# A hybrid decoder layer: the state-space outputs by channels instead of by tokens

## The chip, the cores and the metric

The kernel runs on one core of a Trainium2 chip. The metric is the device time of one execution in microseconds (us).

## What is computed

One layer over 256 tokens of width 2048, in f32. The part that matters here is the state-space (SSD) group with its gate and norm:

```python
z, xbc, dt_raw, q, k, v = jnp.split(a_in @ w_in[i], [o1, o2, o3, o4, o5], axis=-1)
xbc = jax.nn.silu(_causal_dwconv(xbc, conv_w[i], conv_b[i]))
xs, bm, cm = jnp.split(xbc, ...)
dt = jax.nn.softplus(dt_raw + dt_bias[i])
# _ssd: 2 chunks of 128 tokens, 4 groups, 8 heads of 64 channels a group, state 128
y_diag = jnp.einsum('bgecls,bcsgep->bclgep', cb[:, :, None] * decay_in, X)    # X = xs * dt
y_off  = jnp.einsum('bclgn,bcgepn,bgecl->bclgep', Cc, prev, jnp.exp(a_cs))    # state carried in
y = y_diag + y_off + d_skip * xs_h
y = y.reshape(b, s, SSM_INNER) * jax.nn.silu(z)
y_ssm = _rmsnorm(y by 4 groups of 512, ssm_norm_g)
h = h + jnp.concatenate([y_ssm, y_att], axis=-1) @ w_out[i]
```

Behind it come sliding-window attention (the other half of the output projection), a feed-forward part with a convolution, and a gated embedding.

## The kernel before, in words

Every large product is a GEMM over 512 output columns. Its weights come from HBM through the SP queue, 128 x 1024 values at a time, into one of seven tiles `w`. ScalarE (ACT) casts each to a high part `wh` (L192), VectorE (DVE) subtracts to get the low part `wl` (L193), and TensorE (PE) makes three products of 128 x 512 for each slice of the contraction and each block of 128 tokens (L222 to L224). The sum stands in a pair of PSUM tiles, one for each token block, of which there are two pairs. One chunk of the input projection is eight weight tiles of twelve matmuls.

The order in which each engine gets its instructions is made ahead of the run by a planner, which follows the order of the listing where operands are ready by its own costs. The attention stage's matmuls stand in an order written by hand.

At the start the kernel projects B and C of all groups (512 columns each) and the steps dt. Then, in the listing, B and C are evacuated, convolved and put through SiLU (L424 to L429), and behind them comes the steps' chain (L431 to L474): softplus, the decay's cumulative sums, and their store to a scratch tensor `scr`, from which each group loads its rows broadcast over the partitions (`seg`, L481).

For each of four groups, `ssd_x` makes the decay matrices `seg`, multiplies them by C times B (`cb`), projects and convolves x (`xc`, by channels on the partitions), transposes `xc` to have tokens on the partitions, and scales it to `Xd`. The result `yc` is a tile for each token block, tokens on the partitions and 512 channels along it: D skip (L518), plus eight head products of 64 columns (L534), plus, in the second block, the product with the carried state `prev` (L538), scaled by `eacs`. `ssd_gate` projects z and takes its SiLU. `ssd_end` multiplies, sums the squares by rows (L558), scales by the inverse root (L561), and transposes the result back to channels on the partitions (L272), where it is split in high and low parts for the output projection (L195, L196). Group 0 is projected at once, groups 1 to 3 in the attention stage (`output`). `add_to_h` adds each product to the residual stream (L396).

In the listing of the loop, `ssd_end(g)` stands ahead of `ssd_x(g + 1)`.

Transposing by a DMA is in use already, in the attention and the feed-forward part: GpSimd (POOL) sorts the 16-bit halves of f32 values apart (`half`, L881), the SP queue issues the transfer `flip` (L883), and POOL puts the halves together again (L884).

Of the kernel before, what the change touches and what calls it, by code (L numbers as in the profile page):

```python
# [11 lines left out]
F32 = mybir.dt.float32  # L12
# [8 lines left out]
P = 128  # L21
# [44 lines left out]
def hybrid_layer(  # L66
# [330 lines left out]

    def next_lhs(lhs, ss, n, gain):

# [7 lines left out]
        V.tensor_reduce(out=s1, in_=ss, axis=AX.X, op=ALU.add)  # L407
        return rstd(s1, D, NB, tag)

    def project(lhs, w, i0, ni, after=None):  # L410

        for n in range(4):
            acc = acc_pair()
            gemm(acc, lhs, [w[i, n] for i in range(i0 * KG // KW, (i0 + ni) * KG // KW)])
            add_to_h(acc, n)
            if after:
                after(n)

# [2 lines left out]
    with tc.tile_pool(name="ssd", bufs=1) as sp, tc.tile_pool(name="dram", bufs=1, space=bass.MemoryType.DRAM) as dp:  # L421
        BT = sb(sp, [P, 4, T], "BT")
        CT = sb(sp, [P, 4, T], "CT")
        for c, (acc, dst, tag) in enumerate(((acc_b, BT, "ct"), (acc_c, CT, "Xd"))):  # L424
            t = evac_scaled(acc, sp, tag, 1)
            if c == 0:
                S.copy(dtT, dt_ps[:64, :T])
            conv_chunk(t, dst, scw, 4, 16 + 4 * c)
            S.activation(out=dst, in_=dst, func=AF.Silu)  # L429

        tr = tr_tile()  # L431
        for b in range(NB):
            PE.matmul(tr[:, b * 32 : (b + 1) * 32], lhsT=dtT[:, b * P : (b + 1) * P], rhs=sel, start=True, stop=True)
# [36 lines left out]
        V.tensor_copy(acsT, ps[:64, :P])  # L470
        scr = dp.tile([64, P], F32, tag="scr", name="scr")
        nc.sync.dma_start(scr, acsT)
        eacs = sb(sp, [P, 64], "eacs")
        S.activation(out=eacs, in_=acs, func=AF.Exp)  # L474

        def ssd_x(g):
            segs = []
            for c in range(NB):
                hs = slice(g * 16 + c * 8, g * 16 + c * 8 + 8)
                seg = sb(sp, [P, 8, P], "seg", bufs=3)  # L480
                nc.sync.dma_start(seg, scr[hs, :].partition_broadcast(P))  # L481
# [4 lines left out]
                V.tensor_tensor(out=seg, in0=seg, in1=bc(acs[:, hs], P), op=ALU.subtract)  # L486
                G.affine_select(
                    out=seg, in_=seg, compare_op=ALU.is_ge, fill=-1.0e30, base=0, pattern=[[0, 8], [1, P]], channel_multiplier=-1
                )
                S.activation(out=seg, in_=seg, func=AF.Exp)  # L490
                segs.append(seg)
# [20 lines left out]
            y, Xd = [], []  # L512
# [13 lines left out]
            PE.matmul(st, lhsT=Bt, rhs=xe, start=True, stop=True)  # L526
            prev = sb(sp, [P, NC], "prev")
            S.copy(prev, st)
            for c in range(NB):
                yc = y[c]  # L530
                yp = ms_tile()
                for h in range(8):
                    hs = slice(h * HD, (h + 1) * HD)
                    PE.matmul(yp[:, hs], lhsT=segs[c][:, h, :], rhs=Xd[c][:, hs], start=True, stop=True)  # L534
                V.tensor_tensor(out=yc, in0=yc, in1=yp, op=ALU.add)
                if c:
                    off = ms_tile()
                    PE.matmul(off, lhsT=CT[:, g, c * P : (c + 1) * P], rhs=prev, start=True, stop=True)  # L538
                    t = sb(sp, [P, NC], "xe")
                    o = g * 16 + 8  # L540
                    V.tensor_tensor(out=v3(t, 8), in0=v3(off, 8), in1=bc(eacs[:, o : o + 8], HD), op=ALU.mult)
                    V.tensor_tensor(out=yc, in0=yc, in1=t, op=ALU.add)
            return y

        def ssd_gate(g):
            acc = in_chunk(3 + 2 * g)
            zs = []
            for b in range(NB):
                z = sb(sp, [P, NC], f"z{b}")
                S.activation(out=z, in_=acc[b], func=AF.Silu, scale=rx[:, b : b + 1])  # L550
                zs.append(z)
            return zs

        def ssd_end(g, y, zs):
            ssy = sb(sp, [P, NB], "ssy", bufs=2)
            for b in range(NB):
                V.tensor_tensor(out=y[b], in0=y[b], in1=zs[b], op=ALU.mult)
                S.activation(out=zs[b], in_=y[b], func=AF.Square, accum_out=ssy[:, b : b + 1])  # L558
            ry = rstd(ssy, NC, NB, "ry")
            for b in range(NB):  # L560
                V.tensor_scalar_mul(y[b], y[b], ry[:, b : b + 1])  # L561
# [5 lines left out]
        zs = ssd_gate(0)  # L567

        with tc.tile_pool(name="rope", bufs=1) as rp:
            posf = sb(rp, [P, NB], "posf")  # L570
# [53 lines left out]
        fill(const)  # L624

        for g in range(4):
            held[g] = ssd_end(g, y, zs)
            if g < 3:
                y = ssd_x(g + 1)
                zs = ssd_gate(g + 1)  # L630
            if g < 1:
                project(*held.pop(g))


    ms_.close()
# [2 lines left out]
    with tc.tile_pool(name="att_s", bufs=2) as as_, tc.tile_pool(name="att", bufs=2, reuse_waits="tile") as ap_, tc.tile_pool(name="ps_sc", bufs=1, space=PSUM) as ps_sc:  # L638
# [130 lines left out]
        def values(j):  # L769

            yT = Lhs(yp_, KG, "y")
            for b in range(NB):
# [16 lines left out]
            held[4 + j] = (yT, w_out, 4 + j, 1)  # L789

        def chunk(c, then):
            acc = acc_pair()
# [5 lines left out]
                yield  # L798

        def output(i):  # L800
            lhs, w, i0, ni = held.pop(i)
            for n in range(4):
                acc = acc_pair()
                for s in range(2):
                    products(acc, lhs, load_w(w[i0 * 2 + s, n]), s * KW, KW, KG, s == 1)
                    if s == 1:
                        add_to_h(acc, n)
                    yield

        at = {}  # L810
# [190 lines left out]
```

## Time and profile before

| | us |
|---|---|
| median of three runs | 1434.23 (1433.61 to 1436.1) |
| the profiled execution | 1436.61 |
| its span, first to last instruction | 1434.9 |
| PE busy | 1423.2 (99%) |
| PE weight loads (PEld) busy | 1167.3 (81%) |
| DVE busy | 984.1 (69%) |
| ACT busy | 804.2 (56%) |
| POOL busy | 286.2 (20%) |

Busy time is the union of an engine's instructions. Matmuls are pipelined, so their listed durations overlap and add up to more than the time. A row of a group gives line, engine, operation, the names of output and inputs, the shapes, the count; then the busy time and the mean duration in ns of one, and the idle time just before them with what ended it. In a row of a stretch stand its limits and length, the busy time and count for PE, PEld, DVE, ACT and POOL, the granted clock of PE, the DMA share and GB/s. A row in order of time gives start, duration, engine, line and count. A row of waits gives the total, the number and the longest.

### The profile page before, as it was taken

How to read it: one execution, taken by the hardware profiler on the slowest of the kernel's cores; microseconds unless marked ns; L12 is line 12 of the kernel's file. 1: busy time of each engine (PE TensorE's matmuls, PEld its weight loads, DVE VectorE, ACT ScalarE, POOL GpSimd, SP SyncE). 2: the span in 40 equal slices, each digit the busy share in tenths (PEclk: the TensorE clock that was granted, in tenths of full speed). 3: DMA queues.
4: the chain of work that ended last, by engine and by line, in shares of the span. 5: the costliest groups of instructions: out<-in, count | busy, mean ns of one | idle time of the engine just before them, and what ended most of it. 6: DMA issues, size and time to landing. Idle time of an engine off the chain costs nothing.

```text
span 1434.9 us, 18092 instructions
## 1 busy us (share of the span) xinstructions
PE 1423.2 (99%) x6527; PEld 1167.3 (81%) x6527; DVE 984.1 (69%) x1242; ACT 804.2 (56%) x1101; POOL 286.2 (20%) x212
## 2 busy tenths in 40 slices
PE   9999999999999999999999999999999999999998
PEld 7887888888787778888888888888888888888887
DVE  6678876776678897656667646765675576476854
ACT  6675555644567666556556446545554554455643
POOL 0002010008345432013243112201320131120000
PEclk9999999999999999999999999999999999999999
DMA  9656656548687778577887767867876877776671
GB/s 332 236 173 198 215 177 185 171 148 223 188 220 187 209 220 220 168 211 207 219 226 202 217 205 206 225 196 198 230 208 192 223 201 218 206 208 190 208 226 65
DMA packets 163467, 292.62 MB, mean 204 GB/s; under 512 B 93041, under 2 KB 95921, under 8 KB 162993
## 3 DMA queue, kind: packets, MB, share of 16 engines
q1 hardware_dynamic: 162944, 290.99, 70.5%
q8 instruction: 51, 0.84, 0.2%
q10 hardware_dynamic: 432, 0.48, 0.1%
q14 instruction: 40, 0.32, 0.1%
HBM read 268.32 MB, written 2.13 MB: 188 GB/s over the span
## 4 chain that ended last, share of the span: by engine, by line
PE 68%; DVE 1%; ACT 0%; issue 0%; POOL 0%; DVEq 0%; ACTq 0%
PE acc L222 22%; PE acc L224 22%; PE acc L223 22%; PE tr L779 1%; PE tr L272 0%; PE sc L738 0%; DVE wl L193 0%; ACT s L753 0%; DVE nm L749 0%; DVE s L742 0%; ACT wh L192 0%; DVE sg L931 0%; ACT s L761 0%; DVE qkr L672 0%; DVE h L396 0%
## 5 line engine op out<-in xcount | busy, mean ns | idle before, releaser
L193 DVE TENSOR_TENSOR wl<-w,wh 128x1024 fp32r<-128x1024 f32 (+1 forms) x495 | 634.9, 1288 | 378.5 <-ACT wh L192 376.4
L192 ACT CAST wh<-w 128x1024 fp32r<-128x1024 f32 (+1 forms) x495 | 514.8, 1045 | 480.7 <-PE acc L224 431.4
L223 PE MATMUL acc<-wl,ah 128*128 128x512 f32 x1278 | 500.1, 391 | 1.5 <-DVE wl L193 1.5
L224 PE MATMUL acc<-wh,al 128*128 128x512 f32 x1278 | 499.0, 391 | 0.0
L222 PE MATMUL acc<-wh,ah 128*128 128x512 f32 x1278 | 498.3, 392 | 0.0
L223 PEld LDWEIGHTS acc<-wl,ah 128*128 128x128 f32 x1278 | 240.1, 188 | 52.3 <-DVE wl L193 2.4
L222 PEld LDWEIGHTS acc<-wh,ah 128*128 128x128 f32 x1278 | 240.1, 188 | 51.0 <-issue 1.4
L224 PEld LDWEIGHTS acc<-wh,al 128*128 128x128 f32 x1278 | 240.1, 188 | 50.1 <-issue 0.7
L224 PE MATMUL acc<-wh,gl 128*128 128x512 f32 x352 | 137.1, 390 | 0.0
L223 PE MATMUL acc<-wl,gh 128*128 128x512 f32 x352 | 137.1, 390 | 0.0
L222 PE MATMUL acc<-wh,gh 128*128 128x512 f32 x352 | 136.5, 390 | 0.0
L881 POOL COPY half<-u 128x1024 uint16<-128x1024 uint16 x44 | 62.0, 1422 | 264.3 <-ACT u L879 264.3
L222 PE MATMUL acc<-wh,yh 128*128 128x512 f32 x256 | 101.6, 397 | 0.6 <-DVE h L396 0.6
L223 PE MATMUL acc<-wl,yh 128*128 128x512 f32 x256 | 99.9, 390 | 0.0
L224 PE MATMUL acc<-wh,yl 128*128 128x512 f32 x256 | 99.7, 390 | 0.0
L884 POOL COPY uc<-flip 128x1024 uint16<-128x1024 uint16 x44 | 54.9, 1248 | 177.2 <-DMA flip<-half 174.9
L223 PEld LDWEIGHTS acc<-wl,gh 128*128 128x128 f32 x352 | 66.1, 188 | 13.7
L224 PEld LDWEIGHTS acc<-wh,gl 128*128 128x128 f32 x352 | 66.1, 188 | 13.6
L222 PEld LDWEIGHTS acc<-wh,gh 128*128 128x128 f32 x352 | 66.1, 188 | 13.6
L288 DVE SCALAR_TENSOR_TENSOR cv<-uc,fcw,cv 128x254 f32<-128x254 f32 (+1 forms) x176 | 73.2, 476 | 3.4 <-ACT cv L286 3.4
L396 DVE TENSOR_TENSOR h<-h,acc 128x512 f32<-128x512 f32 x112 | 73.0, 678 | 1.8 <-PE acc L224 1.8
L222 PEld LDWEIGHTS acc<-wh,yh 128*128 128x128 f32 x256 | 48.1, 188 | 14.6 <-issue 2.0
(239 smaller groups left out, 1129.2 us busy)
## 6 DMA issues: line engine op xcount, KB each, us to landing
w<-in_w_up_dram SPq DMA_DIRECT2D x176, 512.0 KB, 4.2
w<-in_w_in_dram SPq DMA_DIRECT2D x126, 512.0 KB, 4.2
w<-in_w_down_dram SPq DMA_DIRECT2D x88, 512.0 KB, 4.3
w<-in_w_out_dram SPq DMA_DIRECT2D x64, 512.0 KB, 4.2
w<-in_w_pg_dram SPq DMA_DIRECT2D x32, 512.0 KB, 4.3
seg<-scr SPq DMA_DIRECT2D x8, 512.0 KB, 5.0
xt<-in_xT_dram SPq DMA_DIRECT2D x16, 128.0 KB, 7.0
h<-in_x_dram SPq DMA_DIRECT2D x2, 1024.0 KB, 8.7
```

Source lines behind the costliest of these rows:

```text
L192: S.copy(hi, src)
L193: V.tensor_tensor(out=lo, in0=src, in1=hi.bitcast(F32), op=ALU.subtract)
L222: PE.matmul(acc[b], lhsT=hi, rhs=wh[:, i, :], start=(k == 0), stop=False)
L223: PE.matmul(acc[b], lhsT=hi, rhs=wl[:, i, :], start=False, stop=False)
L224: PE.matmul(acc[b], lhsT=lo, rhs=wh[:, i, :], start=False, stop=(k == total - 1 or (b == NB - 1 and k + 1 == whole)))
L288: V.scalar_tensor_tensor(out=dst[:, s:], in0=ps[:, : T - s], scalar=taps[n - 1 - s], in1=dst[:, s:], op0=ALU.mult, op1=ALU.add)
L396: V.tensor_tensor(out=hs, in0=hs, in1=acc[b], op=ALU.add)
L779: PE.matmul(v3(o[e * HD : (e + 1) * HD, kv * 2 * P : (kv + 1) * 2 * P], 2), lhsT=v[kb][:, vs], rhs=pT[e][:, :, kb, :], start=(kb == 0), st ...
L881: G.tensor_copy(half.rearrange("p (a n) -> p a n", a=2), u_.bitcast(U16).rearrange("p (n a) -> p a n", a=2))
L884: G.tensor_copy(uc[:, :, b * P : (b + 1) * P].bitcast(U16).rearrange("p f (t a) -> p f t a", a=2), flip.rearrange("p (a f) t -> p f t a", ...
```

## The change

The result of a group, `y`, now has channels on the partitions (`[128, 4, 256]`). A head's product takes a 64-column slice of `Xd` as weights and the decay matrix as the moving operand (128 columns); the two heads of a pair write the lower and upper 64 partitions of one PSUM tile. The carried state is added in the same PSUM tile, with `prev` as weights and `grown` (the exponential of the cumulative sums times C) as moving operand. D skip is one fused pass by channel over `xc`, which is in that layout already. z of groups 0 to 2 is turned to that layout with two flips through the SP queue; group 3's z is transposed on PE. The sum of squares over channels is a product with a column of ones, and the inverse root is applied when the projection is added to h. The steps' chain is listed ahead of the convolutions of B and C, and `ssd_x(g + 1)` ahead of `ssd_end(g)`.

```diff
-    def add_to_h(acc, n):
+    def add_to_h(acc, n, scale=None):
         for b in range(NB):
             hs = hres[b][:, n * NC : (n + 1) * NC]
-            V.tensor_tensor(out=hs, in0=hs, in1=acc[b], op=ALU.add)
+            if scale is None:
+                V.tensor_tensor(out=hs, in0=hs, in1=acc[b], op=ALU.add)
+            else:
+                V.scalar_tensor_tensor(out=hs, in0=acc[b], scalar=scale[:, b : b + 1], in1=hs, op0=ALU.mult, op1=ALU.add)
...
-        for c, (acc, dst, tag) in enumerate(((acc_b, BT, "ct"), (acc_c, CT, "Xd"))):
-            t = evac_scaled(acc, sp, tag, 1)
-            if c == 0:
-                S.copy(dtT, dt_ps[:64, :T])
-            conv_chunk(t, dst, scw, 4, 16 + 4 * c)
-            S.activation(out=dst, in_=dst, func=AF.Silu)
-
+        bt = evac_scaled(acc_b, sp, "ct", 1)
+        S.copy(dtT, dt_ps[:64, :T])
         tr = tr_tile()
...
         nc.sync.dma_start(scr, acsT)
-        eacs = sb(sp, [P, 64], "eacs")
-        S.activation(out=eacs, in_=acs, func=AF.Exp)
+        for c, (t, dst) in enumerate(((bt, BT), (None, CT))):
+            t = t or evac_scaled(acc_c, sp, "Xd", 1)
+            conv_chunk(t, dst, scw, 4, 16 + 4 * c)
+            S.activation(out=dst, in_=dst, func=AF.Silu)
+        skip = sb(sp, [P, 16], "skip")
+        for e_ in range(2):
+            es = slice(e_ * HD, (e_ + 1) * HD)
+            V.tensor_copy(skip[es, :], dsk[es, :].rearrange("p (f e) -> p e f", e=2)[:, e_, :])
+        ones = nc.const_aps.tensor(1.0, [P, 1], F32)
...
                     S.activation(out=dec, in_=dec, func=AF.Exp)
+                else:
+                    grown = sb(sp, [P, 8, P], "grown")
+                    S.activation(out=grown, in_=seg, func=AF.Exp)
+                    V.tensor_tensor(
+                        out=grown, in0=grown, in1=CT[:, g, P:].unsqueeze(1).to_broadcast([P, 8, P]), op=ALU.mult
+                    )
...
-                yc = sb(sp, [P, NC], f"yc{b}", bufs=2)
-                V.tensor_tensor(out=v3(yc, 8), in0=v3(tr, 8), in1=bc(dsk[:, g * 8 : (g + 1) * 8], HD), op=ALU.mult)
-                y.append(yc)
...
-            for c in range(NB):
-                yc = y[c]
-                yp = ms_tile()
-                for h in range(8):
-                    hs = slice(h * HD, (h + 1) * HD)
-                    PE.matmul(yp[:, hs], lhsT=segs[c][:, h, :], rhs=Xd[c][:, hs], start=True, stop=True)
-                V.tensor_tensor(out=yc, in0=yc, in1=yp, op=ALU.add)
-                if c:
-                    off = ms_tile()
-                    PE.matmul(off, lhsT=CT[:, g, c * P : (c + 1) * P], rhs=prev, start=True, stop=True)
-                    t = sb(sp, [P, NC], "xe")
-                    o = g * 16 + 8
-                    V.tensor_tensor(out=v3(t, 8), in0=v3(off, 8), in1=bc(eacs[:, o : o + 8], HD), op=ALU.mult)
-                    V.tensor_tensor(out=yc, in0=yc, in1=t, op=ALU.add)
+            y = sb(sp, [P, 4, T], "y", bufs=2)
+            for half in range(2):
+                yp = ms_tile().rearrange("p (a t) -> p a t", a=2)
+                own = [(0, i, Xd[0], segs[0]) for i in range(2)]
+                for i in range(2):
+                    own += [(1, i, Xd[1], segs[1]), (1, i, prev, grown)]
+                for c, i, left, right in own:
+                    for e_ in range(2):
+                        h = 4 * half + 2 * i + e_
+                        PE.matmul(
+                            yp[e_ * HD : (e_ + 1) * HD, i, c * P : (c + 1) * P],
+                            lhsT=left[:, h * HD : (h + 1) * HD],
+                            rhs=right[:, h, :],
+                            start=(left is not prev),
+                            stop=(left is not Xd[1]),
+                            skip_group_check=True,
+                        )
+                for i in range(2):
+                    f = 2 * half + i
+                    V.scalar_tensor_tensor(
+                        out=y[:, f, :], in0=xc[:, f, :], scalar=skip[:, 4 * g + f : 4 * g + f + 1], in1=yp[:, i, :], op0=ALU.mult, op1=ALU.add
+                    )
             return y
 
         def ssd_gate(g):
...
-            return zs
+            if g == 3:
+                return zs
+            zT = sb(sp, [P, 4, T], "zT")
+            for b in range(NB):
+                half = sb(sp, [P, 2 * NC], f"half{b}", U16)
+                G.tensor_copy(half.rearrange("p (a n) -> p a n", a=2), zs[b].bitcast(U16).rearrange("p (n a) -> p a n", a=2))
+                flip = zs[b].bitcast(U16).rearrange("p (a t) -> p a t", a=8)
+                nc.sync.dma_start_transpose(flip, half)
+                G.tensor_copy(
+                    zT[:, :, b * P : (b + 1) * P].bitcast(U16).rearrange("p f (t a) -> p f t a", a=2),
+                    flip.rearrange("p (a f) t -> p f t a", a=2),
+                )
+            return zT
 
-        def ssd_end(g, y, zs):
-            ssy = sb(sp, [P, NB], "ssy", bufs=2)
-            for b in range(NB):
-                V.tensor_tensor(out=y[b], in0=y[b], in1=zs[b], op=ALU.mult)
-                S.activation(out=zs[b], in_=y[b], func=AF.Square, accum_out=ssy[:, b : b + 1])
-            ry = rstd(ssy, NC, NB, "ry")
-            for b in range(NB):
-                V.tensor_scalar_mul(y[b], y[b], ry[:, b : b + 1])
-            yT = Lhs(yp_, KG, "y")
-            transpose_split(y, yT, 0, g_ssm[:, 4 * g : 4 * g + 4])
-            return (yT, w_out, g, 1)
+        def ssd_end(g, y, z):
+            if g < 3:
+                V.tensor_tensor(out=y, in0=y, in1=z, op=ALU.mult)
+            else:
+                for half in range(2):
+                    fs = slice(2 * half, 2 * half + 2)
+                    tr = tr_tile().rearrange("p (a t) -> p a t", a=2)
+                    for i in range(2):
+                        f = 2 * half + i
+                        for b in range(NB):
+                            PE.transpose(tr[:, i, b * P : (b + 1) * P], z[b][:, f * P : (f + 1) * P], ident)
+                    V.tensor_tensor(out=y[:, fs, :], in0=y[:, fs, :], in1=tr, op=ALU.mult)
+            yT = Lhs(yp_, KG, "y")
+            for f in range(4):
+                split(y[:, f, :], *yT.part(f), g_ssm[:, 4 * g + f : 4 * g + f + 1])
+            sq = z if g < 3 else sb(sp, [P, 4, T], "zT")
+            S.activation(out=sq, in_=y, func=AF.Square)
+            V.tensor_tensor(out=sq[:, :2, :], in0=sq[:, :2, :], in1=sq[:, 2:, :], op=ALU.add)
+            s1 = sq[:, 0, :]
+            V.tensor_tensor(out=s1, in0=s1, in1=sq[:, 1, :], op=ALU.add)
+            ps = ms_tile()
+            for b in range(NB):
+                PE.matmul(ps[:, b : b + 1], lhsT=s1[:, b * P : (b + 1) * P], rhs=ones, start=True, stop=True)
+            return yT, w_out, g, 1, rstd(ps[:, :NB], NC, NB, f"ry{g}")
...
         for g in range(4):
-            held[g] = ssd_end(g, y, zs)
+            y_next = ssd_x(g + 1) if g < 3 else None
+            held[g] = ssd_end(g, y, z)
+            y = y_next
             if g < 3:
-                y = ssd_x(g + 1)
-                zs = ssd_gate(g + 1)
+                z = ssd_gate(g + 1)
```

`project` and `output` pass the group's scale on to `add_to_h`; attention's parts pass none.

More of the change, by code (lines that the diff above doesn't have):

```diff
@@ L408, in finish_rstd, with project @@
         return rstd(s1, D, NB, tag)
-    def project(lhs, w, i0, ni, after=None):
+    def project(lhs, w, i0, ni, after=None, scale=None):
         for n in range(4):
@@ L414, in project @@
             gemm(acc, lhs, [w[i, n] for i in range(i0 * KG // KW, (i0 + ni) * KG // KW)])
-            add_to_h(acc, n)
+            add_to_h(acc, n, scale)
             if after:
@@ L511, in ssd_x @@
             S.activation(out=xc, in_=xc, func=AF.Silu)
-            y, Xd = [], []
+            Xd = []
             for b in range(NB):
@@ L560, in ssd_end @@
             for b in range(NB):
-                V.tensor_scalar_mul(y[b], y[b], ry[:, b : b + 1])
-            yT = Lhs(yp_, KG, "y")
-            transpose_split(y, yT, 0, g_ssm[:, 4 * g : 4 * g + 4])
-            return (yT, w_out, g, 1)
+                PE.matmul(ps[:, b : b + 1], lhsT=s1[:, b * P : (b + 1) * P], rhs=ones, start=True, stop=True)
+            return yT, w_out, g, 1, rstd(ps[:, :NB], NC, NB, f"ry{g}")
         y = ssd_x(0)
-        zs = ssd_gate(0)
+        z = ssd_gate(0)
         with tc.tile_pool(name="rope", bufs=1) as rp:
@@ L626, in hybrid_layer @@
         for g in range(4):
-            held[g] = ssd_end(g, y, zs)
+            y_next = ssd_x(g + 1) if g < 3 else None
+            held[g] = ssd_end(g, y, z)
+            y = y_next
             if g < 3:
-                y = ssd_x(g + 1)
-                zs = ssd_gate(g + 1)
+                z = ssd_gate(g + 1)
             if g < 1:
-                project(*held.pop(g))
+                lhs, w, i0, ni, scale = held.pop(g)
+                project(lhs, w, i0, ni, scale=scale)
     ms_.close()
@@ L788, in values @@
                 split(v3(o, 4), hi, lo)
-            held[4 + j] = (yT, w_out, 4 + j, 1)
+            held[4 + j] = (yT, w_out, 4 + j, 1, None)
         def chunk(c, then):
@@ L800, in output @@
         def output(i):
-            lhs, w, i0, ni = held.pop(i)
+            lhs, w, i0, ni, scale = held.pop(i)
             for n in range(4):
@@ L806, in output @@
                     if s == 1:
-                        add_to_h(acc, n)
+                        add_to_h(acc, n, scale)
                     yield
```

## The prediction

> **What bounds the kernel now.** I read the page's engine shares first, then its costliest groups, then the grouped rows by stretch, the waits of TensorE, and last the order of time around the small matmuls that the change replaces.
>
> ```profile
> span 1434.9 us, 18092 instructions
> ...
> PE 1423.2 (99%) x6527; PEld 1167.3 (81%) x6527; DVE 984.1 (69%) x1242; ACT 804.2 (56%) x1101; POOL 286.2 (20%) x212
> ...
> L193 DVE TENSOR_TENSOR wl<-w,wh 128x1024 fp32r<-128x1024 f32 (+1 forms) x495 | 634.9, 1288 | 378.5 <-ACT wh L192 376.4
> L192 ACT CAST wh<-w 128x1024 fp32r<-128x1024 f32 (+1 forms) x495 | 514.8, 1045 | 480.7 <-PE acc L224 431.4
> ```
>
> TensorE (PE) is busy 99% of the span, and the weight stream waits for it: the cast of a weight tile (L192) waits 431 us in total for PE to give back a buffer. So the time is the sum of what each matmul takes of PE's stream, plus PE's few stalls. What a matmul takes is not its listed duration, because matmuls are pipelined; it is the distance to the next start.
>
> ```profile
> 700.00:800.00 100.00, 100.00 (x443) 82.86 (x442) 68.29 (x75) 56.62 (x69) 34.00 (x21) 1.00 0.83 225
> 50.00:330.00 280.00, 277.58 (x1341) 229.15 (x1340) 205.14 (x294) 161.58 (x211) 23.66 (x19) 1.00 0.57 179
> ```
>
> In a stretch of nothing but large 128x512 matmuls, 443 of them fill 100 us, 0.226 us each, under full load of the flips of the feed-forward part. The second row is the stage that the change touches (the state-space groups): VectorE (DVE) has 75 us of 280 idle, ScalarE (ACT) 118, GpSimd (POOL) 256. The stalls of PE in this stage are small:
>
> ```profile
> PE acc L223 <- DVE wl L193: 1.5, 2, 1.0
> PE tr L299 <- issue: 0.9, 1, 0.9
> ```
>
> **The change part by part.** PE first, since only PE's sum sets the end. Each f32 matmul leaves two records; a transpose leaves one. The price of a run of small matmuls is the distance from its start to the next large one, plus what that next one takes above 0.23.
>
> The removed head products (L534) and the removed product with the carried state (L538):
>
> ```profile
> 125.24 1.89 PE L534 MATMUL ms<-Xd,seg 128*128 128x64 f32 x16
> 126.94 0.47 PE L223 MATMUL acc<-wl,ah 128*128 128x512 f32 x1
> 127.26 0.39 PE L224 MATMUL acc<-wh,al 128*128 128x512 f32 x1
> ```
> ```profile
> 128.87 1.02 PE L538 MATMUL ms<-prev,CT 128*128 128x512 f32 x2
> 129.32 0.80 PE L222 MATMUL acc<-wh,ah 128*128 128x512 f32 x1
> 129.96 0.40 PE L223 MATMUL acc<-wl,ah 128*128 128x512 f32 x1
> ```
> ```profile
> L534 PE MATMUL ms<-Xd,seg 128*128 128x64 f32 x128 | 15.1, 272 | 0.0
> ```
>
> Eight heads of one chunk take 1.70 + 0.09 = 1.79 us. There are two chunks and four groups: 8 x 1.79 = 14.3 us (the grouped row has 15.1 with the tails of each run). The carried state takes 0.45 + 0.41 = 0.86 us, four times: 3.4 us.
>
> The removed transposes of the result, 8 a group, in groups 0 to 2 (group 3 transposes z instead, the same 8):
>
> ```profile
> 145.43 1.03 PE L272 MATMUL tr<-ident,yc 128*128 128x128 f32 x8
> 146.22 0.47 PE L223 MATMUL acc<-wl,ah 128*128 128x512 f32 x1
> 146.53 0.39 PE L224 MATMUL acc<-wh,al 128*128 128x512 f32 x1
> ```
>
> 0.79 + 0.08 = 0.87 us, three times: 2.6 us. Together PE loses 14.3 + 3.4 + 2.6 = 20.3 us of work.
>
> Added are 24 products a group, with weights of 64 columns, 128 moving columns, and the two heads of a pair writing partitions 0-63 and 64-127. No such product is in the trace at this size, but the attention's L779 has the same 64-column weights and the same two output halves with 256 moving columns, and L738 has pairs on the two row halves with 128:
>
> ```profile
> 485.37 0.39 PE L224 MATMUL acc<-wh,yl 128*128 128x512 f32 x1
> 485.69 2.81 PE L779 MATMUL tr<-s,v 128*64 128x256 f32 x24
> 488.43 0.51 PE L222 MATMUL acc<-wh,yh 128*128 128x512 f32 x1
> 488.77 0.40 PE L223 MATMUL acc<-wl,yh 128*128 128x512 f32 x1
> ```
> ```profile
> 371.95 1.16 PE L738 MATMUL sc<-kT,qT 64*128 64x128 f32 x16 [1.37 <-POOL qT L689]
> 373.04 0.50 PE L222 MATMUL acc<-wh,ah 128*128 128x512 f32 x1
> 373.38 0.39 PE L223 MATMUL acc<-wl,ah 128*128 128x512 f32 x1
> ```
>
> A 128-column record takes 0.11 us alone (8 transposes in 0.87), so 24 records of 256 columns one after another would take 24 x 0.22 = 5.3 us. They took 2.74: the two halves run side by side, 12 pairs at 0.214 (= 2.57). Around that lie 0.09 before, 0.17 within and 0.11 after, so one visit to the split array costs 0.37 us. L738's 8 pairs took 1.09 + 0.11; at 0.107 to 0.111 a pair this leaves 0.31 to 0.34, and with the same 0.09 ahead, which its wait hides, 0.40 to 0.43. I take 0.111 a pair and 0.40 a visit. A group has 48 records, 24 pairs; four groups 96 x 0.111 = 10.7 us.
>
> How many visits? The products are listed as two halves of a PSUM tile each. The first pairs (chunk 0) need no carried state; the later ones need `prev`, which comes behind the state's matmul and a copy on ACT. So I expect PE to be sent in once before `prev` is there and once behind it: two a group, 8 x 0.40 = 3.2 us. Ends: one a group (1.6 us) and one for every change of operand, six a half (48 visits, 19.2 us).
>
> Last, the sum of squares over the channels: two products with a column of ones, four records a group with 128-column weights. Nearest row:
>
> ```profile
> 103.19 0.61 PE L495 MATMUL ms<-CT,BT 128*128 128x128 f32 x4
> 103.55 0.48 PE L222 MATMUL acc<-wh,ah 128*128 128x512 f32 x1
> ```
>
> 0.36 + 0.09 = 0.45 us for four records with 128 columns; a single column can hardly take more, and no row excludes nearly nothing. I take 0.45, 1.8 us in all, since L534's records with 64 columns took the same 0.11 as these with 128. The Trainium skill, TensorEngine Tiling (Array Packing), Instruction Overhead, puts the least cost of a small matmul at about 60 cycles; by that rule, at the skill's 2.4 GHz, the sixteen records would come to an estimated 0.4 us and the sum below to 1.4 us less. No row here shows a single-column matmul.
>
> PE's sum: -20.3 + 10.7 + 3.2 + 1.8 = **-4.6 us**.
>
> **The other engines**, which have to stay hidden:
>
> ```profile
> L535 DVE TENSOR_TENSOR yc<-yc,ms 128x512 f32<-128x512 f32 x8 | 5.5, 682 | 4.2 <-PE ms L534 4.2
> L561 DVE TENSOR_SCALAR yc<-yc,ry 128x512 f32<-128x512 f32 x8 | 3.5, 479 | 1.5 <-POOL ry L187 1.5
> L196 DVE SCALAR_TENSOR_TENSOR yl<-tr,gains,yh 128x256 fp32r<-128x256 f32 x16 | 7.1, 476 | 1.3 <-ACT yh L195 1.3
> L497 DVE TENSOR_TENSOR seg<-seg,ms 128x1024 f32<-128x1024 f32 x8 | 9.4, 1208 | 0.0
> L490 ACT ACTIVATE seg<-seg 128x1024 f32<-128x1024 f32 x8 | 8.5, 1062 | 18.7 <-POOL seg L487 18.7
> L558 ACT ACTIVATE z<-yc 128x512 f32<-128x512 f32 x8 | 5.0, 629 | 9.2 <-DVE yc L557 9.2
> ```
>
> DVE loses, per group, eight passes of 512 columns (two D-skip products, two sums, two for the carried state, two gates) at 0.68 and two scalings at 0.48: 6.4 us. It gains four fused skips of 256 columns at 0.48, the product of `grown` and C at 1.21, one gate of 1024 columns at 1.21 and two sums of squares, 0.68 and, by its width, about 0.4: 5.4 us. The splits stay. So DVE is relieved by about 1 us a group. ACT trades two squares of 0.63 for one of 1.06 and gains one Exp of 1.06: about 1 us a group more, in 118 us of idle time. The scaled sums into h (eight in the projection of group 0, 24 in the attention stage) are one pass over the same 512 columns as before; I cost them at nothing, since the pass count is what DVE pays for and nothing waits longer.
>
> The flips of z, two in each of groups 0 to 2, bring two POOL copies and one SP transfer each:
>
> ```profile
> L881 POOL COPY half<-u 128x1024 uint16<-128x1024 uint16 x44 | 62.0, 1422 | 264.3 <-ACT u L879 264.3
> L884 POOL COPY uc<-flip 128x1024 uint16<-128x1024 uint16 x44 | 54.9, 1248 | 177.2 <-DMA flip<-half 174.9
> ```
> ```profile
> DMA to landing us min/median/max: 3.8/5.4/7.5
> ```
> ```profile
> SPq L883 <- POOL half L881: 13.4, 17, 1.5
> ```
>
> Six flips cost POOL 6 x 2.67 = 16 us of its 256 idle. From the end of a z chunk to zT it is 0.7 (Silu) + 1.4 + 5.4 + 1.2, twice and partly overlapped: 9 to 14 us, while the next x chunk keeps PE for eight weight tiles x 12 matmuls x 0.226 = 21.7 us. On the SP queue the weight loads stand behind a flip that waits for its half; the same transfer waited at most 1.5 us in the feed-forward part, and seven weight buffers of 2.7 us each cover up to 19. If that cover were gone, each flip would cost PE its wait, some 1.5 us.
>
> The moved chain (softplus, cumulative sums, the store to `scr` on SP and what they issue) is work of 64 columns that exists in both; it comes earlier by the two convolutions. Behind its store on SP stand weight loads, under the same cover. Behind it on ACT stands the evacuation of C's accumulator, which is wanted only when the z chunk begins, a chunk (21.7 us) later. Where it helps is here:
>
> ```profile
> DVE seg L486 <- DMA seg<-scr: 4.8, 1, 4.8
> ```
>
> DVE stood 4.8 us for a load of decay rows that belongs to group 1, and the 1.0 us stall of PE follows it. The first stall of PE (0.5) comes in the burst of group 0's decay work, which the moved chain spreads. Both may go (-1.5) or new ones may come with three waits of DVE for zT (at 1.0 each, +3). I take 0.
>
> **The sum.** The profiled execution took 1436.61 us (span 1434.9): 1436.6 - 4.6 = 1432.0. The median of the three runs is 1434.23, 2.4 below it, and the work removed is the same there: **1429.6 us**, 0.32% faster. A difference of less than 0.2% (2.9 us) can't be told from none here.
>
> **Rivals.**
>
> *More than the sum.* One visit a group and no DVE stall: -4.6 - 1.6 - 1.5 = -7.7, 1426.5 us. For it: the operands of chunk 0 may well come as late as `prev`, since L534 ran just ahead of L538. Against: two visits are the listed order. 0.22.
>
> *The gain is eaten by new waits.* DVE waits in order for zT, or SP for a half, and the weight split behind it comes late three times at 1.0 to 1.5 us: -4.6 + 3 to 4.5, 1432.6 to 1434.1 us. For it: one late load already did that. Against: 44 flips in the feed-forward part without a stall. 0.22.
>
> *Too many visits (slower).* The place is the two halves of `yp`: if the order puts large matmuls between the single products, each return costs 0.40. The saving before visits is 20.3 - 10.7 - 1.8 = 7.8 us, so from 20 visits the gain is gone and from 27 it is slower by over 0.2%; with 32 (four a half) +5.0, 1439.2 us. For it: groups of operands become ready at different times. Against: L534 kept its 16 records together. 0.10.
>
> *The halves don't run side by side (slower).* Then 192 records at 0.107 take 20.5 instead of 10.7: +5.2, 1439.4 us. The rows of L779 speak against it, at twice the width. The Trainium skill, TensorE: Matmul & The Clock Gate, Part 3, says that weight loads overlap running matmuls only where the row group differs; column halves share theirs, so by that rule the loads would be exposed here. By that rule L779 could not have kept 0.214 a pair; the trace disagrees. 0.04.
>
> **How the numbers follow.** The forecast, 1427.5 to 1431.3, has 0.42. Faster by over 0.2%: 0.42 + 0.22 = 0.64. Within: the eaten gain, 0.22. Slower: 0.10 + 0.04. The range goes from 1425.5 (the larger gain and the ones at nothing) to 1437.5, where a few visits too many reach; about 0.15 is left out, most of it above.
>
> **What would show it.** In the changed profile: no rows of L534 and L538; 192 records of 64-column weights and 128 columns, in runs whose pairs start together and follow at 0.11; the count of those runs (8 forecast); sixteen records with the ones at 0.11; 24 fewer transposes in the groups; PE's waits in the stage still near 2.4 us. More runs than 20, records that follow singly, or waits of PE for weight splits behind a gate with zT would make the forecast wrong.

## The result and the profile after

| | before | after |
|---|---|---|
| median (lowest to highest), us | 1434.23 (1433.61 to 1436.1) | 1447.81 (1446.44 to 1449.46) |
| profiled execution, us | 1436.61 | 1449.46 |
| span, us | 1434.9 | 1447.7 |

The ratio is 1.0093 [1.0075, 1.011]: slower by 13.6 us, where 4.6 us less was forecast.

The engine shares of the changed kernel's page hardly differ from those of before:

```profile
PE 1421.6 (98%) x6575; PEld 1161.7 (80%) x6575; DVE 997.0 (69%) x1237; ACT 805.3 (56%) x1091; POOL 297.1 (21%) x224
```

TensorE is busy 1.6 us less and the span is 12.8 us longer, so the time went into TensorE's waits. The four largest of them in the changed kernel, over the whole run (total, number, longest):

```profile
PE acc L222 <- DVE h L400: 13.1, 4, 11.5
PE sc L786 <- POOL qT L737: 2.1, 1, 2.1
PE ms L510 <- ACT CT L475: 1.7, 1, 1.7
PE acc L223 <- DVE wl L193: 1.5, 1, 1.5
...
```

One wait of 11.5 us is most of the loss. It is for L400, the add of group 0's projection into h. The stretches of 50 us, as before (limits, length, busy time of PE, PEld, DVE, ACT and POOL, granted clock, DMA share, GB/s), place it; the first row is the kernel before, the second the changed one:

```profile
150.00:200.00 50.00, 50.00 (x245) 41.43 (x244) 38.29 (x53) 27.04 (x35) 3.38 (x2) 1.00 0.60 190
150.00:200.00 50.00, 37.97 (x201) 30.85 (x200) 37.01 (x49) 22.68 (x27) 8.14 (x7) 0.86 0.58 164
```

Before, this stretch of TensorE was full, at a clock of 1.00. TensorE's rows there in the changed kernel, in order of time:

```profile
173.90 0.61 PE L609 MATMUL ms<-const-float32-1.0,zT 128*128 128x1 f32 x4
...
175.03 0.68 PE L510 MATMUL ms<-CT,BT 128*128 128x128 f32 x4 [0.53 <-DVE rs_t L185]
187.20 0.80 PE L222 MATMUL acc<-wh,yh 128*128 128x512 f32 x1 [11.48 <-DVE h L400]
187.79 0.63 PE L223 MATMUL acc<-wl,yh 128*128 128x512 f32 x1
...
190.78 0.40 PE L224 MATMUL acc<-wh,yl 128*128 128x512 f32 x1
```

Both pairs of PSUM tiles hold finished products of group 0 and no add has freed one. After the wait eight matmuls take 3.58 us instead of 1.82 (0.43 us apart behind the first, instead of 0.23), another 1.8 us. VectorE's rows of the same time say what it did instead of the adds:

```profile
174.80 0.15 DVE L185 TENSOR_SCALAR rs_t<-ms 128x2 f32<-128x2 f32 x1
175.75 1.22 DVE L512 TENSOR_TENSOR seg<-seg,ms 128x1024 f32<-128x1024 f32 x1 [0.80 <-PE ms L510]
...
180.75 1.23 DVE L498 TENSOR_TENSOR grown<-grown,CT 128x1024 f32<-128x1024 f32 x1 [3.77 <-ACT grown L497]
181.89 1.22 DVE L501 TENSOR_TENSOR seg<-seg,acs 128x1024 f32<-128x1024 f32 x1
183.02 0.16 DVE L493 TENSOR_TENSOR dec<-seg,acs 128x8 f32<-128x8 f32 x1
183.22 2.13 DVE L501 TENSOR_TENSOR seg<-seg,acs 128x1024 f32<-128x1024 f32 x1
185.27 1.21 DVE L589 TENSOR_TENSOR y<-y,zT 128x1024 f32<-128x1024 f32 x1
186.41 1.40 DVE L400 SCALAR_TENSOR_TENSOR h<-acc,ry,h 128x512 f32<-128x512 f32 x2
```

The scale `ry` of group 0 comes from the ones product at 173.90, behind group 1's head products. VectorE makes its first step, `rs_t`, at 174.80, and GpSimd the second, behind its two copies that put group 1's z together:

```profile
174.57 2.25 POOL L580 COPY zT<-z 128x1024 uint16<-128x1024 uint16 x2 [13.28 <-PE ms L609]
176.78 0.71 POOL L187 TENSOR_TENSOR ry<-rs_t,nhalf 128x2 f32<-128x2 f32 x1
```

So the scale was there at 177.49, 8.9 us before the first add. In VectorE's order the adds stand behind the decay passes of the next groups and behind group 1's gate (L589). VectorE moreover stands 3.77 us for `grown`, whose exponential waits on ScalarE for a late load of decay rows:

```profile
ACT L497 <- DMA seg<-scr: 6.6, 1, 6.6
```

In that idle time, from 176.97 to 180.75, all four adds (2.7 us) would have fitted behind the scale. It is their place in the order, more than the scale's own time, that kept them back.

For a balance I take the starts of the 193rd, 1301st and 2201st large matmul (55, 347 and 582 us before; the state-space stage and the attention stage) and split the distance into 0.227 us for each large matmul, the waits, the small matmuls by the forecast's pricing, and the rest (half rate, mostly). In us, of one profiled execution each:

| | state-space stage: total | waits | small matmuls | rest | attention stage: total | waits |
|---|---|---|---|---|---|---|
| before | 291.6 | 1.5 | 37.5 | 1.1 | 235.7 | 3.2 |
| after | 302.6 | 15.5 | 32.9 | 2.6 | 238.1 | 3.7 |
| after less before | +11.0 | +14.0 | -4.5 | +1.5 | +2.4 | +0.5 |

So the small matmuls did what was forecast, and the waits took three times as much back.

### The profile page after: what moved, and what is told of

Same layout as the page of the kernel before. It is cut to its first block, busy times and chain, and to the rows that moved or that the text cites. A ratio compares the mean times of both kernels' runs of the same rounds, so it can differ in the third digit from the quotient of the medians.

```text
span 1447.7 us, 18205 instructions
## 1 busy us (share of the span) xinstructions
PE 1421.6 (98%) x6575; PEld 1161.7 (80%) x6575; DVE 997.0 (69%) x1237; ACT 805.3 (56%) x1091; POOL 297.1 (21%) x224
## 3 DMA queue, kind: packets, MB, share of 16 engines
HBM read 268.32 MB, written 2.13 MB: 187 GB/s over the span
## 4 chain that ended last, share of the span: by engine, by line
PE 66%; DMA 0%; DVE 0%; ACT 0%; issue 0%; POOL 0%; SPq 0%; DVEq 0%; POOLq 0%; ACTq 0%
PE acc L222 22%; PE acc L223 21%; PE acc L224 21%; PE tr L827 1%; PE tr L272 0%; DMA flip<-half 0%; PE sc L786 0%; POOL qT L737 0%; DVE sg L979 0%; DVE wl L193 0%; ACT wh L192 0%; SPq L207 0%; DVE sg L980 0%; ACT half L813 0%; ACT s L809 0%
## 5 line engine op out<-in xcount | busy, mean ns | idle before, releaser
L224 PEld LDWEIGHTS acc<-wh,gl 128*128 128x128 f32 x352 | 66.1, 188 | 13.6
L224 PEld LDWEIGHTS acc<-wh,yl 128*128 128x128 f32 x256 | 48.5, 189 | 10.4
```

The source lines that it names most:

```text
L224: PE.matmul(acc[b], lhsT=lo, rhs=wh[:, i, :], start=False, stop=(k == total - 1 or (b == NB - 1 and k + 1 == whole)))
```

## The experiments

Three theories for the 11.5 us. A: the adds need the scale, the scale comes late, and the planner therefore puts the adds far back on VectorE. B: the late decay rows, for which VectorE stands, whatever the scale does. C: the flips of z, whose result the gate L589 needs. Each kernel starts from the changed one unless it says otherwise; ratios are to the kernel before, run on the same chip. "Later" stands for the edit under "Group 0 projected one group later".

**The scale left out for group 0**

```diff
-                project(lhs, w, i0, ni, scale=scale)
+                project(lhs, w, i0, ni)
```

> Group 0's projection is added to h without its scale (this leaves out group 0's norm factor); all else as in the changed kernel. Theory A (the scale of group 0 comes too late, so its adds stand far back in VectorE's queue and TensorE runs out of PSUM pairs): the 11.5 us wait of TensorE on the adds goes, and with it some 1.8 us of half-rate matmuls behind it: 1447.8 - 13.3 = about 1434.5 us. Theory B (VectorE is held by group 2's decay rows, whatever the scale does): the wait stays above 8 us, about 1447 us. Theory C (the flips of z come late): no change, 1447.8 us.

Measured: 1429.63 us, ratio 0.9971 [0.9962, 0.9981]. This kernel's waits of TensorE:

```profile
PE ms L510 <- ACT CT L475: 1.7, 1, 1.7
PE acc L223 <- DVE wl L193: 1.5, 1, 1.5
...
```

No wait for the adds is left (without a scale they are L398), although the flips and the late decay rows are still there. VectorE stands even longer for `grown`, now behind the adds:

```profile
187.69 1.80 DVE L498 TENSOR_TENSOR grown<-grown,CT 128x1024 f32<-128x1024 f32 x1 [4.49 <-ACT grown L497]
```

So A carries the wait; B and C alone make none. (That the time equals the forecast's is luck: 0.6 us come from the state-space stage, 290.9 for 291.6, and 4.1 from attention, 231.6 for 235.7, where this execution had no wait at all.)

**The ones product in the other PSUM rotation**

```diff
-            ps = ms_tile()
+            ps = tr_tile()
```

> The products with the ones take their PSUM tile from the transposes' pool instead of the pool that the head products of the next group use; listing order unchanged. Theory A, in the form that the scale is late because its PSUM tile stands behind group 1's products in a rotation of two: the first products with the ones start near 153 us instead of 174, the wait on the adds goes, about 1434.5 us. Theory B: the wait stays above 8 us, about 1447 us. Theory C: no change.

Measured: 1438.08, 1.0026 [1.0016, 1.0035].

```profile
PE acc L222 <- DVE h L400: 4.5, 3, 3.3
...
```

VectorE's rows from 177 us on:

```profile
177.13 1.22 DVE L589 TENSOR_TENSOR y<-y,zT 128x1024 f32<-128x1024 f32 x1
178.27 2.72 DVE L400 SCALAR_TENSOR_TENSOR h<-acc,ry,h 128x512 f32<-128x512 f32 x4
```

`rs_t` comes at 170.4 instead of 174.8, and the adds now stand ahead of the pass of `grown` (182.06): the longest wait falls from 11.5 to 3.3. An earlier scale moved the adds forward in VectorE's order.

**`ssd_end(g)` ahead of `ssd_x(g + 1)` again, without and with the other rotation**

```diff
-            y_next = ssd_x(g + 1) if g < 3 else None
             held[g] = ssd_end(g, y, z)
-            y = y_next
             if g < 3:
+                y = ssd_x(g + 1)
                 z = ssd_gate(g + 1)
```

> The loop's listing order is put back: ssd_end(g) ahead of ssd_x(g + 1); all else as in the changed kernel. Theory A: group 0's tile for the ones is then asked for ahead of group 1's, its scale comes before its adds are due, no wait on them over 1 us: about 1434 us, 1430 if the attention stage also loses its new waits. Theory B: the decay rows of group 2 still hold VectorE in front of the adds: about 1445 us. Theory C: 1447 us.

> Both edits of the two kernels before it: listing order put back and the ones in the transposes' PSUM pool. Theory A: no better than either alone in this wait (it is gone already), so within 2 us of them, about 1433 us. Theory B or C: above 1444 us.

Measured: 1437.53, 1.0028 [1.0018, 1.0038], and 1440.46, 1.0048 [1.0033, 1.0063]. The waits of the first:

```profile
PE acc L223 <- DVE wl L193: 6.3, 3, 4.1
...
PE acc L222 <- DVE h L400: 0.6, 1, 0.6
```

The long wait for the adds is gone, and one for weight splits has come in its place: group 0's gate now stands on VectorE ahead of them, with its splits and the next group's decay passes. The second has a short state-space stage (290.8), and pays it back in attention (240.4), where TensorE waits 4.3 us for qT and then runs at half rate (a granted clock of 0.50 up to 378.7 us).

**Group 0 projected one group later**

```diff
-            if g < 1:
-                lhs, w, i0, ni, scale = held.pop(g)
+            if g == 1:
+                lhs, w, i0, ni, scale = held.pop(0)
                 project(lhs, w, i0, ni, scale=scale)
```

> Group 0's projection is listed one turn of the loop later (behind group 2's z chunk); all else as in the changed kernel, its scale included. Theory A: its scale is long there when its adds are due, so the wait of 11.5 us is gone with the whole computation in place, 1430 to 1434.5 us. Theory B (VectorE held by the decay rows of the group that is one ahead): a wait of 3 us or more on the adds comes back one turn later, 1438 us or more.

Measured: 1436.1, 1.0009 [0.9999, 1.0019]. Its runs lie between 1432.3 and 1438.8, so the median alone says little; the waits say more:

```profile
PE acc L223 <- DVE wl L193: 2.7, 3, 1.6
...
PE ms L510 <- ACT CT L475: 1.7, 1, 1.7
...
PE acc L222 <- DVE h L400: 0.6, 1, 0.6
```

The large wait goes with the full scaling in place, so A is confirmed without leaving anything out. The time only comes back to that of the kernel before: the saving of 4.6 us isn't there yet. What is left are waits of 1 to 2 us, of which the one for C's convolution (L475) belongs to the moved chain.

**The moved chain by itself**

Three kernels: the changed one with the convolutions of B and C ahead of the chain again; the kernel before with the chain moved ahead; and the first with "later".

```diff
         S.copy(dtT, dt_ps[:64, :T])
+        for c, (t, dst) in enumerate(((bt, BT), (None, CT))):
+            t = t or evac_scaled(acc_c, sp, "Xd", 1)
+            conv_chunk(t, dst, scw, 4, 16 + 4 * c)
+            S.activation(out=dst, in_=dst, func=AF.Silu)
...
         nc.sync.dma_start(scr, acsT)
-        for c, (t, dst) in enumerate(((bt, BT), (None, CT))):
-            t = t or evac_scaled(acc_c, sp, "Xd", 1)
-            conv_chunk(t, dst, scw, 4, 16 + 4 * c)
-            S.activation(out=dst, in_=dst, func=AF.Silu)
```

> The steps' chain is listed behind the convolutions of B and C again, as in the kernel before; all else as in the changed kernel. If the moved chain costs TensorE its wait of 1.7 us on C's convolution near 98 us, that wait goes, and about 1446 us stay with the wait on the adds. If the moved chain is what brings the adds' wait, 1434 us. If it helps, as its listing ahead would suggest, 1450 us.

> The kernel before with the steps' chain ahead of the convolutions and nothing else of the change. If the move costs a wait on C's convolution and saves VectorE's stall of 0.5 us: 1435 to 1437 us, with a wait of TensorE on CT of 1 to 2 us. If it only saves: 1433.5 us.

> The projection of group 0 one turn later and the steps' chain behind the convolutions; all else as in the changed kernel. Theory A with a costly chain: the least waits of all, 1427 to 1430 us (the forecast's saving of 4.6 us and no new wait). If the chain's place is harmless: the same as the kernel with the later projection alone. Theory B: above 1436 us.

Measured: 1449.31, 1.0103 [1.0087, 1.0118]; 1440.98, 1.0049 [1.0032, 1.0066]; 1435.51, 1.001 [0.9994, 1.0025]. The first still waits for the adds (11.8 us in three, the longest 9.6), but no longer for CT. In the second the wait for CT comes up without anything else of the change; its state-space stage is 0.7 us shorter (290.9) and its attention stage 4.6 longer:

```profile
PE sc L737 <- POOL qT L688: 4.8, 1, 4.8
PE ms L494 <- ACT CT L473: 1.0, 1, 1.0
```

The third loses the wait for CT and gets 3.3 us for weight splits, the longest 2.6. So the moved chain exchanges one small wait for another, and isn't the cause of the loss.

**A fourth decay tile**

```diff
-                seg = sb(sp, [P, 8, P], "seg", bufs=3)
+                seg = sb(sp, [P, 8, P], "seg", bufs=4)
```

Room for it: `prev` shares a tile with `xe`, and the two `half` tiles are one.

> The changed kernel with four tiles for the decay matrices instead of three (room made by letting prev use xe's tile and the two halves of z share one). Group 2's rows can then be loaded once group 0's products are done, some 40 us earlier, and VectorE isn't held by that load. If the wait of 11.5 us is part late load, part place in VectorE's queue: it shrinks by the 4 to 6 us that VectorE stood for the load, to 5 to 7 us, and the time to about 1442 us. If only the scale's lateness counts: it stays above 9 us, 1447 us. If the load was all of it: below 2 us, 1435 us.

Measured: 1443.97, 1.0067 [1.0044, 1.009]; the longest wait for the adds is 7.9 us. VectorE's rows:

```profile
177.12 1.70 DVE L498 TENSOR_TENSOR grown<-grown,CT 128x1024 f32<-128x1024 f32 x1
178.74 2.17 DVE L501 TENSOR_TENSOR seg<-seg,acs 128x1024 f32<-128x1024 f32 x1
180.83 1.21 DVE L512 TENSOR_TENSOR seg<-seg,ms 128x1024 f32<-128x1024 f32 x1
...
182.58 1.22 DVE L501 TENSOR_TENSOR seg<-seg,acs 128x1024 f32<-128x1024 f32 x1
183.72 1.22 DVE L589 TENSOR_TENSOR y<-y,zT 128x1024 f32<-128x1024 f32 x1
184.86 2.72 DVE L400 SCALAR_TENSOR_TENSOR h<-acc,ry,h 128x512 f32<-128x512 f32 x4
```

VectorE doesn't stand for `grown` any more, and still the adds come at 184.86, behind an unbroken row of passes. Against the changed kernel the wait is 3.6 us shorter, about the 3.77 of standing: that is B's part. The other 7.9 stay with A; here the scale itself came at 181.47, so the order and the late scale share them.

**"Later" with z transposed on TensorE in all groups, and with the other rotation and the convolutions ahead of the chain**

```diff
-            if g == 3:
+            if True:
                 return zs
...
-            if g < 3:
+            if False:
                 V.tensor_tensor(out=y, in0=y, in1=z, op=ALU.mult)
...
-            sq = z if g < 3 else sb(sp, [P, 4, T], "zT")
+            sq = sb(sp, [P, 4, T], "zT")
```

> The projection of group 0 one turn later, and z transposed on TensorE in all groups instead of by flips (24 transposes more, 2.6 us by the rows of the kernel before). If the flips bring waits (theory C), the waits of TensorE shrink by more than 2.6 us against the kernel with the later projection alone, below 1434 us. If not, 1437 to 1440 us.

> Three edits on the changed kernel: the projection of group 0 one turn later, the steps' chain behind the convolutions, the ones in the transposes' PSUM pool. The work on TensorE is as forecast, 4.6 us less than before; whatever its waits exceed those of the kernel before is lost again. Between 1429.6 (waits as before) and 1436 us (as the kernel with the first two edits).

Measured: 1433.81, 0.9996 [0.9987, 1.0005], and 1438.88, 1.0031 [1.002, 1.0042]. Without flips the waits for weight splits (2.7 us with "later") are gone and the state-space stage's waits fall from 4.4 to 1.9, while the 24 transposes raise its small matmuls from 32.7 to 35.0. By these two the flips cost about what they save. The stage as a whole is 2.5 us shorter (289.2 for 291.7): "later" ran at a clock of 0.50 from 101.2 to 104.4 us, behind its wait for CT, and this kernel, with the same wait, at 1.00. The median is 2.3 us lower too and just under the 1434 us that the expectation set for theory C, so a small cost of the flips isn't excluded. The large wait isn't theirs, since "later" lost it with the flips in place; C falls for that one. The other rotation, which helped where the scale was urgent, no longer does; TensorE then waits for weight splits (4.4 us in five) and for the evacuation `ct` (2.5), and why it loses I can't say from these rows.

**All together: "later", the convolutions ahead of the chain, four decay tiles**

> The projection of group 0 one turn later, the steps' chain behind the convolutions, four tiles for the decay matrices. VectorE isn't held by decay rows in any group: waits as in the kernel before or below, 1428 to 1431 us. If the remaining waits (VectorE's weight split near 141 us, the queries' flips in attention) have another cause: about 1435 us.

> The kernel before with four tiles for the decay matrices instead of three and nothing else. If the gain of the best version (1430.0 us) is the smaller work on TensorE, this one has only VectorE's wait of 4.8 us on a late load to win, 0 to 1.5 us: 1433 to 1434.5 us. If the fourth tile brings the gain, 1430 us.

> The best version (1430.0 us) with the steps' chain ahead of the convolutions, as the change has it. If the moved chain costs TensorE its wait of 1.7 us on C's convolution and saves nothing: 1432 us. If it spreads VectorE's load in group 0 and so takes away the waits of 1.8 and 1.7 us on weight splits: 1428 to 1429 us.

Measured: 1430.02 (1429.43 to 1430.11), ratio 0.9967 [0.9955, 0.998], faster than both kernels. The fourth tile in the kernel before, without the rest: 1442.34, 1.0049 [1.0032, 1.0066]. With the moved chain: 1430.9, 0.9985 [0.9965, 1.0004].

The waits of the first:

```profile
PE acc L223 <- DVE wl L193: 3.5, 2, 1.8
...
PE acc L222 <- DVE h L400: 0.6, 1, 0.6
```

Its state-space stage takes 287.9 us: waits 3.5 (+2.0 against before), small matmuls 31.5 (-6.0), the rest 1.4 (+0.3), together -3.7. So the saving that the forecast gave the layout by channels can be had, but it takes both edits. "Later" without the fourth tile is no faster than the kernel before, with the chain in either place (1436.1 and 1435.51; stages of 291.7 and 291.1). The fourth tile by itself leaves the stage as it was (291.8). With both, the ratio falls from 1.0009 to 0.9985 and, with the convolutions ahead of the chain, from 1.001 to 0.9967.

What the fourth tile adds to "later" is seen in that last pair, without it and with it, where VectorE takes up group 1's decay rows:

```profile
135.08 0.17 DVE L493 TENSOR_TENSOR dec<-seg,acs 128x8 f32<-128x8 f32 x1 [4.74 <-DMA seg<-scr]
135.98 0.95 DVE L493 TENSOR_TENSOR dec<-seg,acs 128x8 f32<-128x8 f32 x1 [0.23 <-DMA seg<-scr]
```

Without it VectorE stands 4.74 us for them, TensorE then waits 2.56 us for a weight split, and its clock is at 0.50 from 143.8 to 147.0; with it the longest such wait is 1.8 us and no half rate follows. That the one brings the other is read from these rows, not tested by itself.

One thing stays open. In the kernel before with either single edit (the chain moved, or the fourth tile), and in the one with `ssd_end` first and the other rotation, TensorE waits 4.3 to 4.8 us for qT at the first attention scores. In these three, and in the kernel before (1.4 us), ScalarE begins to evacuate the keys 3.8 to 7.2 us after their chunk has ended; in the twelve others it begins before the chunk's end, and there is no such wait at the first scores. That goes together in all sixteen, but no edit tested it, and the lengths don't go in proportion.

## Why the prediction was wrong, by its steps

**Removed and added work of TensorE: right.** -4.6 us forecast, -4.5 measured. The second visit of group 3 in the changed kernel, TensorE's rows in order of time:

```profile
309.07 0.39 PE L223 MATMUL acc<-wl,ah 128*128 128x512 f32 x1
309.39 0.44 PE L550 MATMUL ms<-grown,prev 128*64 128x128 f32 x4
...
311.19 0.39 PE L550 MATMUL ms<-grown,prev 128*64 128x128 f32 x4
311.51 0.50 PE L224 MATMUL acc<-wh,al 128*128 128x512 f32 x1
311.84 0.39 PE L222 MATMUL acc<-wh,ah 128*128 128x512 f32 x1
...
314.59 0.50 PE L609 MATMUL ms<-const-float32-1.0,zT 128*128 128x1 f32 x4
314.95 0.49 PE L222 MATMUL acc<-wh,ah 128*128 128x512 f32 x1
315.28 0.40 PE L223 MATMUL acc<-wl,ah 128*128 128x512 f32 x1
```

Thirty-six records in 2.12 us, with 0.09 ahead and 0.10 behind: 2.32. That is 18 pairs at 0.107 and 0.39 for the visit, against 0.111 and 0.40 forecast. Visits were seven instead of eight (group 1 takes one less here, group 0 in the best kernel).

The halves of a pair run side by side, and the loads of their weights are hidden: a load's record lasts 0.137 us, and a pair with its two loads takes 0.107. The Trainium skill, TensorE: Matmul & The Clock Gate, Part 3, lets a weight load overlap only where row groups differ; at this size the trace disagrees, as at the attention's.

**The product with ones: right.** 0.36 + 0.10 = 0.46 us for four records, 0.45 forecast. The Trainium skill, TensorEngine Tiling (Array Packing), Instruction Overhead, would have made it an estimated 0.4 us for all sixteen; at 0.46 us for four, 1.8 us for sixteen, the trace disagrees.

**The two slower rivals: neither came.** The kernel did get slower, but not by too many visits (there were seven) or by halves that follow one another.

**New waits, "I take 0", with bounds of -1.5 and +3: the step that failed.** It came to +14.0 in the state-space stage, with 1.5 of half rate behind it. The forecast priced the scaled adds by their pass ("the pass count is what DVE pays for and nothing waits longer"). The pass did cost little more, 0.74 us instead of 0.68. But a pass that could start when the product was in PSUM now also needs `ry`, and group 0 is projected in the same turn in which `ry` is made. Two parts of the change put `ry` back further: `ssd_x(1)` is listed ahead of `ssd_end(0)`, and the ones product shares its PSUM rotation with group 1's products. So the planner set the adds behind some 7 us of passes. Before, the scale was applied to `y` ahead of the transposes (L561), so an add waited for nothing but its product.

The forecast's rival of new waits had the right form (work in order on VectorE, weight split behind it) and the wrong place: it looked at what waits for zT, at 1.0 to 1.5 us a time, and not at what waits for the scale. (The flips do have a small part there: the scale was made behind their copies on GpSimd, 1.8 us later than it could have been by the rows above.) Its price was bounded by waits that the trace of before showed, and a wait for PSUM with both pairs full has no such bound: it lasts until VectorE comes round.

**The moved chain: mis-stated.** C's evacuation was said to be wanted only when the z chunk begins. But CT is read by C times B of group 0 (L510). ScalarE's SiLU for CT, which started at 85.4 us before, starts at 99.4:

```profile
L475 ACT ACTIVATE CT<-CT x1: 1056/1056/1056, 99.4 to 99.4; 128x1024 f32<-128x1024 f32 x1
```

and TensorE waits 1.7 us for it. The wait of VectorE for the decay rows, which was to go, came back larger on ScalarE (6.6 us): a decay tile comes free only with head products (L550), for which SP's queue waits with the load, so an earlier store to `scr` doesn't help there, and the fourth tile does (VectorE no longer stands for `grown` with it). The queue's waits between 120 and 190 us:

```profile
SPq L490 <- PE ms L550: 3.5, 4, 2.1
```

## What to carry to other kernels

When a scaling is moved from a factor to the place where a product is added, ask when the scale is ready against when the PSUM tile must come free, not what the pass costs: an add that empties PSUM is urgent, and an engine that works in order puts it behind everything that is ready sooner. Use the product's result one stage later, or keep late scales out of what is projected at once. Taking the urgent add away need not be enough: here it only brought the time back to that of before, and the saving came when VectorE's wait for decay rows went as well. And a change that lightens the bounding engine is to be followed into every queue in which it adds an operand.

## What the runs showed of the hardware

Half rate came after waits shorter than I had thought. In the kernel without group 0's scale a wait of 1.70 us is followed by matmuls 0.43 us apart, at a granted clock of 0.50 from 101.2 to 104.4 us (TensorE's rows in order of time):

```profile
100.84 1.05 PE L510 MATMUL ms<-CT,BT 128*128 128x128 f32 x4 [1.70 <-ACT CT L475]
101.54 0.77 PE L224 MATMUL acc<-wh,al 128*128 128x512 f32 x1
102.11 0.63 PE L222 MATMUL acc<-wh,ah 128*128 128x512 f32 x1
102.54 0.63 PE L223 MATMUL acc<-wl,ah 128*128 128x512 f32 x1
```

In the changed kernel the same wait, 1.69 us, is followed by full rate. Eight of the profiled kernels have this wait for CT at 1.69 or 1.70 us, and half rate follows it in three of them. The Trainium skill, TensorE: Matmul & The Clock Gate, Part 1, has the clock fall after at least one idle window of about 3.4 us that runs free of the kernel. That equal waits end differently fits a window that runs free; the length doesn't fit.

A pass of 1024 columns on VectorE (L501) took 1.22 us or 2.13 us in the same kernel (rows at 181.89 and 183.22 of the changed kernel above). Beside the slow one GpSimd was at work (L502, 1.09 us from 183.18), beside the fast one it wasn't; no run tests whether that is the cause.
